# A layer normalisation that streams through SBUF: tiles of 10 rows in a ring of 50 in place of tiles of 8 rows in a ring of 48

## The chip, the cores and the metric

One Trainium2 chip, one core of it. The metric is the time of one execution on the device in microseconds (us), as a median over executions. Engines: DVE (VectorE), ACT (ScalarE), POOL (GpSimd), SP (SyncE), and the core's 16 DMA engines, which carry everything between HBM and SBUF.

## The reference

```python
# x: (32, 512, 1024) float32, eps = 1e-5
mean = np.mean(x, axis=-1, keepdims=True)
var = np.var(x, axis=-1, keepdims=True)
return ((x - mean) / np.sqrt(var + eps)).astype(np.float32)
```

There are 16384 vectors of 1024 floats. "A row" below is one vector in each of the 128 partitions: 128 x 4 KB = 0.5 MB. There are 128 such rows, each loaded once and stored once.

## The kernel before

A tile of K rows is loaded by one DMA into a slot of the ring. DVE takes statistics (two instructions per row), POOL combines them in small instructions, ACT takes the root, DVE the reciprocal. ACT then normalises in place, and one DMA stores the slot. Loads are issued from SP, stores from ACT. A later load into the same slot waits for the store.

```python
TILES = (2, 2, 4) + (8,) * 14 + (4, 2, 2)
RING = 48
GROUP = 8
...
    def rows_of(a, row, K):        # each partition gets K vectors that lie side by side in HBM
        return a[row * P : (row + K) * P].rearrange("(p k) d -> p k d", p=P)
...
    def group(xs, G):
        stats = st.tile([P, GROUP, NSUB, 6], fdt, name="stats")
        for k in range(G):
            for s in range(NSUB):
                nc.vector.bn_stats(out=stats[:, k, s, :], in_=xs[:, k, s * BN_MAX : (s + 1) * BN_MAX])
        ...                        # nine small POOL instructions for all G rows at once
        nc.scalar.activation(out=std[:, :G], in_=ss[:, :G], func=AF.Sqrt, bias=eps_t, scale=1.0 / D)
        nc.vector.reciprocal(out=rstd[:, :G], in_=std[:, :G])
        nc.gpsimd.tensor_mul(out=nmr[:, :G], in0=nmean[:, :G], in1=rstd[:, :G])
        for k in range(G):
            nc.scalar.activation(out=xs[:, k, :], in_=xs[:, k, :], func=AF.Identity,
                                 bias=nmr[:, k : k + 1], scale=rstd[:, k : k + 1])
...
        for K, row, pos in place(TILES, RING):
            nc.sync.dma_start(out=ring[:, pos : pos + K, :], in_=rows_of(x2, row, K))
            for g in range(0, K, GROUP):
                G = min(GROUP, K - g)
                group(ring[:, pos + g : pos + g + G, :], G)
            nc.scalar.dma_start(out=rows_of(o2, row, K), in_=ring[:, pos : pos + K, :])
```

What one partition gets of one tile lies side by side in HBM. In the trace it is one packet of K x 4 KB; a tile is 128 packets, 8 on each DMA engine.

## Time and profile before

| | before |
|---|---|
| time, median (lowest to highest of 3) | 318.12 us (318.04 to 318.23) |
| span in the profile | 316.1 us |
| load queue and store queue, share of 16 engines | 49.6% + 49.3% |
| data packets per DMA engine | 320 |
| first data packet starts, last one ends | 1.76, 314.9 us |

Read the row of the 40 slices first: each digit is the busy share of one fortieth of the span, in tenths. The times of packets are from the trace's packet records. The prediction below shows the lines. The chain of waits gives shares of the span to what was waited for last:

```profile
DMA 58%; DVE 17%; ACT 9%; POOL 6%; issue 3%; another core or an unknown queue 3%; ACTq 0%; POOLq 0%; DVEq 0%; SPq 0%
```

### The profile page before, as it was taken

What the parts mean: (1) busy time and instruction counts of PE and PEld (TensorE: products, weight loads), DVE (VectorE), ACT (ScalarE), POOL (GpSimd) and SP (SyncE); (2) the same over time, 40 slices, a digit from 0 to 9 for tenths busy, and PEclk for the clock granted to TensorE, in tenths of its full rate; (3) what the DMA queues carried; (4) which work ended last, traced back from release to release, by engine and by line L of the source; (5) the groups of instructions that cost most, each with busy time, mean ns of one, the idle gap of its engine ahead of it and who ended that gap; (6) DMA issues with size and microseconds to landing.
All of it is one profiled execution on the core that took longest, in us unless ns stands there. A gap on an engine that the chain in (4) does not pass through costs nothing.

```text
span 316.1 us, 794 instructions
## 1 busy us (share of the span) xinstructions
DVE 157.1 (50%) x277; ACT 154.3 (49%) x149; POOL 45.1 (14%) x204
## 2 busy tenths in 40 slices
DVE  2368596547092561916529074190652908363030
ACT  1336296692833809247091561900651956196321
POOL 0420202201102020020200202002020020221120
DMA  7999999999999999999999999999999999999996
GB/s 301 433 399 469 431 416 425 433 427 444 420 448 419 444 419 444 435 427 444 419 448 415 448 424 440 423 448 419 444 423 440 423 435 429 446 428 417 455 411 282
DMA packets 5766, 134.27 MB, mean 425 GB/s; under 512 B 640, under 2 KB 640, under 8 KB 640
## 3 DMA queue, kind: packets, MB, share of 16 engines
q1 hardware_dynamic: 2880, 67.11, 49.6%
q10 hardware_dynamic: 2880, 67.11, 49.3%
q14 instruction: 6, 0.05, 0.0%
HBM read 67.11 MB, written 67.11 MB: 425 GB/s over the span
## 4 chain that ended last, share of the span: by engine, by line
DMA 58%; DVE 17%; ACT 9%; POOL 6%; issue 3%; another core or an unknown queue 3%; ACTq 0%; POOLq 0%; DVEq 0%; SPq 0%
DMA ring<-in_x_dram 32%; DMA out_dram<-ring 27%; DVE stats L75 17%; ACT ring L111 8%; POOL half L64 1%; ACT std L103 1%; POOL dev L97 1%; POOL nmean L87 1%; POOL dev L100 1%; POOL dev L90 1%; POOL dev L96 1%; POOL nmean L67 1%; POOL ss L67 1%; DVE rstd L107 0%
## 5 line engine op out<-in xcount | busy, mean ns | idle before, releaser
L75 DVE BATCH_NORM_STATS2 stats<-ring 128x6 f32<-128x512 f32 x256 | 153.7, 678 | 71.2 <-DMA ring<-in_x_dram 71.2
L111 ACT ACTIVATE ring<-ring,nmr,rstd 128x1024 f32<-128x1024 f32 x128 | 147.0, 1227 | 10.8 <-POOL nmr L109 10.8
L103 ACT ACTIVATE std<-ss,eps_t 128x8 f32<-128x8 f32 (+2 forms) x20 | 6.0, 300 | 143.0 <-POOL ss L67 115.8
L107 DVE RECIPROCAL rstd<-std 128x8 f32<-128x8 f32 (+2 forms) x20 | 3.9, 193 | 77.3 <-ACT std L103 77.3
L64 POOL TENSOR_TENSOR half<-stats 128x16 f32<-128x16 f32 (+2 forms) x20 | 4.5, 226 | 221.0 <-DVE stats L75 221.0
L109 POOL TENSOR_TENSOR nmr<-nmean,rstd 128x8 f32<-128x8 f32 (+2 forms) x20 | 4.0, 202 | 27.2 <-DVE rstd L107 27.2
L97 POOL TENSOR_SCALAR dev<-dev 128x32 f32<-128x32 f32 (+2 forms) x20 | 5.6, 281 | 1.8
L100 POOL TENSOR_TENSOR dev<-dev,stats 128x32 f32<-128x32 f32 (+2 forms) x20 | 4.9, 243 | 1.7
L90 POOL TENSOR_TENSOR dev<-stats,nmean 128x32 f32<-128x32 f32 (+2 forms) x20 | 4.6, 231 | 1.7
L87 POOL TENSOR_SCALAR nmean<-nmean 128x8 f32<-128x8 f32 (+2 forms) x20 | 4.6, 228 | 1.8
L96 POOL TENSOR_TENSOR dev<-dev 128x32 f32<-128x32 f32 (+2 forms) x20 | 4.6, 228 | 1.6
L64 POOL TENSOR_TENSOR half<-dev 128x16 f32<-128x16 f32 (+2 forms) x20 | 4.2, 210 | 1.6
L67 POOL TENSOR_TENSOR nmean<-half 128x8 f32<-128x8 f32 (+2 forms) x20 | 4.0, 199 | 1.6
L67 POOL TENSOR_TENSOR ss<-half 128x8 f32<-128x8 f32 (+2 forms) x20 | 4.0, 199 | 1.6
L103 ACT ACT_TABLE_LOAD x1 | 1.3, 1283 | 0.9 <-DVE eps_t L120 0.9
L120 DVE MEMSET eps_t<- 128x1 f32 x1 | 0.1, 59 | 0.8 <-PEq L143 0.8
L143 POOL MEMSET const-float32-0.0<- 128x1 f32 x1 | 0.1, 98 | 0.2 <-issue 0.2
L143 POOL MEMSET const-uint8-127<- 128x1 uint8 x1 | 0.1, 102 | 0.0
L143 POOL MEMSET const-bfloat16-1.0<- 128x1 bf16 x1 | 0.1, 101 | 0.0
L143 POOL MEMSET const-float32-1.0<- 128x1 f32 x1 | 0.1, 98 | 0.0
## 6 DMA issues: line engine op xcount, KB each, us to landing
ring<-in_x_dram SPq DMA_DIRECT2D x14, 4096.0 KB, 47.3
out_dram<-ring ACTq DMA_DIRECT2D x14, 4096.0 KB, 40.7
ring<-in_x_dram SPq DMA_DIRECT2D x4, 1024.0 KB, 30.8
ring<-in_x_dram SPq DMA_DIRECT2D x2, 2048.0 KB, 27.2
out_dram<-ring ACTq DMA_DIRECT2D x4, 1024.0 KB, 16.7
out_dram<-ring ACTq DMA_DIRECT2D x2, 2048.0 KB, 24.5
```

Source lines behind the costliest of these rows:

```text
L64: nc.gpsimd.tensor_tensor(out=half[:, :G], in0=terms[:, :, 0:2], in1=terms[:, :, 2:4], op=ALU.add)
L67: nc.gpsimd.tensor_tensor(out=o, in0=half[:, :G, 0], in1=half[:, :G, 1], op=ALU.add)
L75: nc.vector.bn_stats(out=stats[:, k, s, :], in_=xs[:, k, s * BN_MAX : (s + 1) * BN_MAX],)
L87: nc.gpsimd.tensor_scalar(out=nmean[:, :G], in0=nmean[:, :G], scalar1=-1.0 / H, scalar2=None, op0=ALU.mult)
L90: nc.gpsimd.tensor_tensor(out=dev[:, :G], in0=mean4, in1=nmean[:, :G].unsqueeze(2).to_broadcast([P, G, H]), op=ALU.add,)
L96: nc.gpsimd.tensor_mul(out=dev[:, :G], in0=dev[:, :G], in1=dev[:, :G])
L97: nc.gpsimd.tensor_scalar(out=dev[:, :G], in0=dev[:, :G], scalar1=float(D // H), scalar2=None, op0=ALU.mult)
L100: nc.gpsimd.tensor_tensor(out=dev[:, :G], in0=dev[:, :G], in1=m2, op=ALU.add)
L103: nc.scalar.activation(out=std[:, :G], in_=ss[:, :G], func=AF.Sqrt, bias=eps_t, scale=1.0 / D)
L107: nc.vector.reciprocal(out=rstd[:, :G], in_=std[:, :G])
L109: nc.gpsimd.tensor_mul(out=nmr[:, :G], in0=nmean[:, :G], in1=rstd[:, :G])
L111: nc.scalar.activation(out=xs[:, k, :], in_=xs[:, k, :], func=AF.Identity, bias=nmr[:, k : k + 1], scale=rstd[:, k : k + 1],)
```

## The change

The intent: fewer and larger packets, fewer DMAs, one combination of statistics per larger group, and more small buffers, so that nothing waits for one.

```diff
-TILES = (2, 2, 4) + (8,) * 14 + (4, 2, 2)
+TILES = (4, 6, 10, 10, 10, 10, 10, 10, 10, 10, 10, 10, 10, 6, 2)
-RING = 48
+RING = 50
-GROUP = 8
+GROUP = 10
+FINE = 6
+LAST = 3
...
-    st = ctx.enter_context(tc.tile_pool(name="st", bufs=4))
+    st = ctx.enter_context(tc.tile_pool(name="st", bufs=3))
+    sm = ctx.enter_context(tc.tile_pool(name="sm", bufs=10))   # all small tiles but stats move here
...
-        for K, row, pos in place(TILES, RING):
+        for t, (K, row, pos) in enumerate(plan):
             nc.sync.dma_start(out=ring[:, pos : pos + K, :], in_=rows_of(x2, row, K))
-            for g in range(0, K, GROUP):
-                G = min(GROUP, K - g)
+            step = FINE if t >= len(TILES) - LAST else GROUP
+            for g in range(0, K, step):
+                G = min(step, K - g)
                 group(ring[:, pos + g : pos + g + G, :], G)
             nc.scalar.dma_start(out=rows_of(o2, row, K), in_=ring[:, pos : pos + K, :])
```

The last three tiles are handled in groups of at most 6 rows. The plan of slots is computed as before, in line.

More of the change, by code (lines that the diff above doesn't have):

```diff
@@ L7 @@
 from concourse._compat import with_exitstack
-TILES = (2, 2, 4) + (8,) * 14 + (4, 2, 2)
-RING = 48
-GROUP = 8
-def place(tiles, ring):
-    plan, row, pos = [], 0, 0
-    for K in tiles:
-        if pos + K > ring:
-            pos = 0
-        plan.append((K, row, pos))
-        row += K
-        pos += K
-    return plan
+TILES = (4, 6, 10, 10, 10, 10, 10, 10, 10, 10, 10, 10, 10, 6, 2)
[3 more added lines that the diff above has]
+LAST = 3
 @with_exitstack
@@ L45 @@
     NSUB = D // BN_MAX
+    H = 2 * NSUB
     assert sum(TILES) * P == N
     rings = ctx.enter_context(tc.tile_pool(name="rings", bufs=1))
-    st = ctx.enter_context(tc.tile_pool(name="st", bufs=4))
+    st = ctx.enter_context(tc.tile_pool(name="st", bufs=3))
+    sm = ctx.enter_context(tc.tile_pool(name="sm", bufs=10))
     fdt = mybir.dt.float32
@@ L62, in pool_sum @@
         G = terms.shape[1]
-        half = st.tile([P, GROUP, 2], fdt, name="half")
+        half = sm.tile([P, GROUP, 2], fdt, name="half")
         nc.gpsimd.tensor_tensor(
@@ L78, in group @@
                 )
-        H = 2 * NSUB
         parts = stats[:, :G].rearrange("p g s (h c) -> p g (s h) c", h=2)
         mean4, m2 = parts[:, :, :, 1], parts[:, :, :, 2]
-        nmean = st.tile([P, GROUP], fdt, name="nmean")
-        dev = st.tile([P, GROUP, H], fdt, name="dev")
-        ss = st.tile([P, GROUP], fdt, name="ss")
+        nmean = sm.tile([P, GROUP], fdt, name="nmean")
+        dev = sm.tile([P, GROUP, H], fdt, name="dev")
+        ss = sm.tile([P, GROUP], fdt, name="ss")
         pool_sum(nmean[:, :G], mean4)
@@ L101, in group @@
         pool_sum(ss[:, :G], dev[:, :G])
-        std = st.tile([P, GROUP], fdt, name="std")
+        std = sm.tile([P, GROUP], fdt, name="std")
         nc.scalar.activation(
@@ L105, in group @@
         )
-        rstd = st.tile([P, GROUP], fdt, name="rstd")
+        rstd = sm.tile([P, GROUP], fdt, name="rstd")
         nc.vector.reciprocal(out=rstd[:, :G], in_=std[:, :G])
-        nmr = st.tile([P, GROUP], fdt, name="nmr")
+        nmr = sm.tile([P, GROUP], fdt, name="nmr")
         nc.gpsimd.tensor_mul(out=nmr[:, :G], in0=nmean[:, :G], in1=rstd[:, :G])
@@ L117, in group @@
             )
+    plan, row, pos = [], 0, 0
+    for K in TILES:
+        if pos + K > RING:
+            pos = 0
+        plan.append((K, row, pos))
+        row += K
+        pos += K
     with tc.manual_schedule():
         nc.vector.memset(eps_t, eps_val)
-        for K, row, pos in place(TILES, RING):
+        for t, (K, row, pos) in enumerate(plan):
             nc.sync.dma_start(out=ring[:, pos : pos + K, :], in_=rows_of(x2, row, K))
-            for g in range(0, K, GROUP):
-                G = min(GROUP, K - g)
+            step = FINE if t >= len(TILES) - LAST else GROUP
+            for g in range(0, K, step):
+                G = min(step, K - g)
                 group(ring[:, pos + g : pos + g + G, :], G)
```

## The prediction

> **What bounds the kernel now.** The page comes first, and in it the row of the 40 slices, because a busy share over the whole span can hide idle stretches.
>
> ```profile
> span 316.1 us, 794 instructions
> DVE 157.1 (50%) x277; ACT 154.3 (49%) x149; POOL 45.1 (14%) x204
> DMA  7999999999999999999999999999999999999996
> DMA packets 5766, 134.27 MB, mean 425 GB/s; under 512 B 640, under 2 KB 640, under 8 KB 640
> q1 hardware_dynamic: 2880, 67.11, 49.6%
> q10 hardware_dynamic: 2880, 67.11, 49.3%
> ```
>
> No compute engine is over 50%. The DMA digit is 9 in 38 of 40 slices. The load queue (q1) and the store queue (q10) together take 49.6 + 49.3 = 98.9% of sixteen engines' span, that is 312.6 us of 316.1. The traffic, 67.11 MB in and 67.11 MB out, is the least that the task allows, and the change leaves it alone. At most about 3.5 us are to be had from filling idle DMA time, and these must be at the ends. The stretches say where:
>
> ```profile
> 2.00:300.00 298.00, 154.39 (x271) 150.52 (x146) 42.89 (x190) 1.00 1.00 431
> 300.00:310.00 10.00, 2.64 (x5) 2.67 (x3) 2.05 (x10) 1.00 0.97 414
> 310.00:316.10 6.10, 0.00 (x0) 0.00 (x0) 0.00 (x0) 1.00 0.60 251
> ```
>
> The last two columns are DMA share and GB/s. From 2 to 300 us the share is 1.00. In the trace's packet records the first data packet starts at 1.76 us and the last ends at 314.9 us. So 1.76 us of start and 1.2 us after the last byte are fixed, and between them lie 313.1 us. In the last slice one engine ends 1.7 us before another.
>
> The chain of waits names compute (DVE 17%, ACT 9%), and one could be misled by it: those pieces are behind a full transfer queue. The queue's own waits show the same: the largest is for stores that free the ring.
>
> ```profile
> SPq L122 <- DMA out_dram<-ring: 215.6, 12, 19.0
> ```
>
> 215.6 us of waiting in that queue cost nothing as long as the DMA share is 1.00. The timeline of the end shows how the two queues share the engines:
>
> ```profile
> 276.54 4.85 DVE L75 BATCH_NORM_STATS2 stats<-ring 128x6 f32<-128x512 f32 x8 [1.52 <-DMA ring<-in_x_dram]
> ...
> 288.65 2.48 DVE L75 BATCH_NORM_STATS2 stats<-ring 128x6 f32<-128x512 f32 x4 [3.24 <-DMA ring<-in_x_dram]
> ...
> 300.78 2.47 DVE L75 BATCH_NORM_STATS2 stats<-ring 128x6 f32<-128x512 f32 x4 [6.54 <-DMA ring<-in_x_dram]
> ...
> 309.08 0.34 ACTq L126 DMA_DIRECT2D out_dram<-ring  x1
> ```
>
> The last two loads, of 2 rows, land 12.11 and 12.13 us apart. The packet records have medians of 309, 611 and 1213 ns for packets of 8, 16 and 32 KB, and each engine has 8 packets in a load. Eight turns of one load packet of 8 KB and one store packet of 32 KB make 8 x (309 + 1213) = 12.2 us. So the queues take turns packet by packet, not byte by byte. The last store is issued at 309.08, while the store before it, by the records, is still moving until 310.8 to 312.4. The tail is bound by transfers too; compute beats it by about 2 us.
>
> **What the Trainium skill says.** "DMA: Bandwidth & Descriptors", section "Queues, rings and completion order": each DMA engine goes round robin over its queues at packet granularity. The trace agrees (12.2 worked out, 12.1 measured). Section "Where 436 GB/s comes from" of the same page: 16 ports x 32 B x 850 MHz = 435.2 GB/s. A 32 KB packet in 1213 ns on 16 engines is 432 GB/s, so the kernel stands at that limit. Section "Anatomy of one DMA — SWDGE (gpsimd) path" gives some 2 us of fixed cost per DMA, most of it the receipt of the last write; these DMAs are of the other kind (hardware queues)[...]. In the middle, share 1.00, it is covered by other transfers. "HBM Reference", section "Specifications (TRN2)": a core alone measures about 425 GB/s, bounded by its DMA engines. The page of this kernel shows 425 GB/s.
>
> **The change, part by part.** There are two ledgers: work on the DMA engines, which sets the time, and compute, which matters only if a queue runs dry.
>
> *Packets.* Before: 20 tiles, 8 packets per engine each way, 320 data packets per engine (64 of 8 KB, 32 of 16, 224 of 32). After: 15 tiles, 240 packets. The durations 309, 611, 1213 lie on a line: about 301 ns per 8 KB and 8 ns per packet. An estimate on that line is 912 ns for 24 KB and 1515 for 40 KB. Before: 64 x 309 + 32 x 611 + 224 x 1213 = 311.0 us per engine. After: 16 x 309 + 16 x 611 + 32 x 912 + 176 x 1515 = 310.5 us (4.9 + 9.8 + 29.2 + 266.6). Gain 0.6 us. Completion writes (9 ns each, 40 per engine before, 30 after) give 0.1 us. Sum: -0.7 us.
>
> *The start.* The first tile has 4 rows in place of 2. Its load takes 2.4 us longer, so it lands near 8.1 us (5.69 before). Its 8 statistics take 4.8 us, the chain to the first normalisation 3.4 us (8.16 to 11.58 in the timeline before) and four normalisations 4.6 us, so the first store is issued near 21 us, not at 13.99. This costs nothing if loads fill the engines: the first five loads have no wait, 40 rows x 1.21 us = 48 us of work (one row of all partitions is 301.3 x 8 / 2 = 1.21 us), the sixth waits only for the first load's semaphore, and the seventh needs the stores of the 4-row and 6-row tiles. The second store is issued near 33 us, and turn by turn (8 x (611 + 1515), then 8 x (912 + 1515)) both have landed near 60 us. By then some 37 of the 50 rows first granted are in. The load queue has 13 rows left and does not run dry.
>
> *The middle.* A 10-row tile in both directions takes 8 x 2 x 1.515 = 24.2 us. DVE needs 12.0 us of statistics plus 3.3 us of idling for its own reciprocal, ACT 11.8 us. Both have 9 us to spare. From landing to store issue: 12.0 + 3.7 + 11.5 = 27.2 us (the 8-row tile took 9.6 + 3.7 + 9.2 = 22.5, 37.51 to 60.03). Five tiles give 121 us per turn of the ring against 24 + 27 + 24 = 75 us needed. The ring is looser per row in neither kernel, and nothing starves. The combined statistics take 10 POOL instructions from 20 groups to 16, some 2.6 us each, off the path. The additional small buffers remove waits that were not seen.
>
> *The tail.* With a load landing every 24.2 us, the last 10-row tile (halves of 6 and 4) lands near 261 us. Its successors' packets of 24 and 8 KB alternate with store packets of 40 KB: 8 x (912 + 1515) = 19.4 us and 8 x (309 + 1515) = 14.6 us, so the loads end near 295 us. Stores end near 290 (last but three), 303, 310 and 312.5 us; they are issued near 264, 284, 298 and 303. Each is issued 5 to 26 us before its turn. Compute stays ahead, with more slack than the 2 us of before.
>
> Sum: 318.1 - 0.7 = 317.4 us.
>
> **The rivals.** *Fewer DMAs pay their fixed cost less often.* Ten DMAs fewer at 2 us would make 298 us, 6% faster. Against it stands the share of 1.00 between 2 and 300 us: such a cost would be idle time there, and only 3.5 us of idling exist. I give it 1%. *The coarser grain opens gaps* (late first store, five slots, 27 us from landing to store): a dry store queue alone costs nothing, since loads then take every turn; both must be dry. If the load queue ran dry before the second store came back, some 5 us would be lost (323); if the tail's last two stores came late, 3 to 5 us. My steps leave 13 rows and 5 us of slack, so 2% for more than 6 us. *Load-only stretches are slower*: the records show load packets of 32 KB at a mean of 1274 ns between 10 and 20 us after the first packet, around the first stores' issue, against 1213 later. This cost the mean engine about 0.75 us. The load-only stretch is longer after, so this could grow by 0.3 to 0.6 us and eat the gain: 317.9. *Packets of 40 KB* could be split or move slower than the line says; 1% on them is 2.7 us (320). Speed near the limit and linearity from 8 to 32 KB speak against it.
>
> **Range and chances.** 317.4 us; the rival of slow load stretches and the 1.7 us spread of the engines at the end make some +-0.8, runs of one kernel spread by 0.2. So 316.7 to 318.5. Faster by over 2% (below 311.8) would need less than the bytes' own time at the limit, 310.7 + 1.8 + 1.2 + 2.0 outside the span = 315.7: 1%. Slower by over 2% (above 324.5): 2%. Within: 97%.
>
> **What would show it right or wrong.** Right: DMA 9 in all inner slices, q1 and q10 with 2160 packets each and together 98 to 99% of a span near 315.4; 40 KB packets near 1515 ns; the first store near 21 us; the last loads 14.6 us apart; the last store issued before its predecessor ends. Wrong: a slice below 9 between the second and the 38th, 40 KB packets far from 1515 ns, or a last store that waits for its normalisation with idle engines.

## The result

318.03 us median (317.89 to 318.50, 4 runs) against 318.18 us (318.04 to 318.56, 4 runs). The ratio is 0.9996, with a 95% interval of 0.9979 to 1.0014: the same. Ratios here are the mean time of one kernel's fast runs over that of the other's fast runs in the same rounds, so not quite the ratio of the medians. The profiled execution was the slowest of the four (318.50).

The page of the changed kernel, the lines that answer to those shown of before:

```profile
span 316.6 us, 712 instructions
DVE 156.5 (49%) x273; ACT 152.6 (48%) x145; POOL 37.5 (12%) x164
DMA  8999999999999999999999999999999999999995
DMA packets 4324, 134.25 MB, mean 424 GB/s; under 512 B 480, under 2 KB 480, under 8 KB 480
q1 hardware_dynamic: 2160, 67.11, 49.6%
q10 hardware_dynamic: 2160, 67.11, 49.1%
DMA 42%; DVE 26%; another core or an unknown queue 14%; POOL 6%; ACT 5%; issue 3%; SPq 0%; DVEq 0%; POOLq 0%
```

The packets of each queue fell from 2880 to 2160, and the digits are 9 in 38 of 40 slices again. The chain of waits now gives DVE 26% where it had 17%, at the same time: that view follows one of several ways back through a full queue. Stretches of the same kernel (columns: stretch, its length, DVE, ACT and POOL busy time, clock, DMA share, GB/s):

```profile
2.00:300.00 298.00, 156.31 (x271) 148.91 (x142) 36.39 (x156) 1.00 1.00 431
300.00:310.00 10.00, 0.17 (x1) 2.67 (x3) 0.91 (x5) 1.00 0.99 428
310.00:316.60 6.60, 0.00 (x0) 0.00 (x0) 0.00 (x0) 1.00 0.46 192
```

From 2 to 300 us the engines moved 431 GB/s, exactly as before. The timeline of the end:

```profile
261.86 7.21 DVE L68 BATCH_NORM_STATS2 stats<-ring 128x6 f32<-128x512 f32 x12 [8.69 <-DMA ring<-in_x_dram]
...
281.24 7.22 DVE L68 BATCH_NORM_STATS2 stats<-ring 128x6 f32<-128x512 f32 x12 [0.89 <-DMA ring<-in_x_dram]
...
295.89 2.47 DVE L68 BATCH_NORM_STATS2 stats<-ring 128x6 f32<-128x512 f32 x4 [4.12 <-DMA ring<-in_x_dram]
...
304.19 0.34 ACTq L127 DMA_DIRECT2D out_dram<-ring  x1
```

The last two loads land 14.65 us apart (14.6 predicted from packets that take turns). The last store is issued at 304.19, while by the packet records the store before it ends between 310.6 and 312.8 on the different engines. The last bytes end at 315.2.

So the result lay in the predicted range, and 0.6 us above its point of 317.4. The range also holds 318.1 to 318.2, the time of no change at all, so lying in it is no sign of a gain. What was to be found out: is compute really off the path, is it packets or DMAs that cost, when do the ends and the ring begin to matter, and where is the 0.7 us that the ledger of packets had promised?

### The profile page after: what moved, and what is told of

Its sections match the earlier page's. It is cut to its first block, busy times and chain, and to the rows that moved or that the text cites. A ratio compares the mean times of both kernels' runs of the same rounds, so it can differ in the third digit from the quotient of the medians.

```text
span 316.6 us, 712 instructions
## 1 busy us (share of the span) xinstructions
DVE 156.5 (49%) x273; ACT 152.6 (48%) x145; POOL 37.5 (12%) x164
## 3 DMA queue, kind: packets, MB, share of 16 engines
q1 hardware_dynamic: 2160, 67.11, 49.6%
q10 hardware_dynamic: 2160, 67.11, 49.1%
## 4 chain that ended last, share of the span: by engine, by line
DMA 42%; DVE 26%; another core or an unknown queue 14%; POOL 6%; ACT 5%; issue 3%; SPq 0%; DVEq 0%; POOLq 0%
DMA ring<-in_x_dram 29%; DVE stats L68 26%; DMA out_dram<-ring 13%; ACT ring L103 4%; POOL half L57 1%; POOL dev L89 1%; ACT std L95 1%; POOL dev L92 1%; POOL dev L82 1%; POOL nmean L79 1%; POOL dev L88 1%; POOL nmean L60 1%; POOL ss L60 1%; DVE rstd L99 0%
## 5 line engine op out<-in xcount | busy, mean ns | idle before, releaser
L95 ACT ACTIVATE std<-ss,eps_t 128x10 f32<-128x10 f32 (+3 forms) x16 | 4.8, 301 | 141.7 <-POOL ss L60 141.7
L57 POOL TENSOR_TENSOR half<-stats 128x20 f32<-128x20 f32 (+3 forms) x16 | 3.7, 233 | 243.2 <-DVE stats L68 243.2
L99 DVE RECIPROCAL rstd<-std 128x10 f32<-128x10 f32 (+3 forms) x16 | 3.3, 204 | 51.7 <-ACT std L95 51.7
L89 POOL TENSOR_SCALAR dev<-dev 128x40 f32<-128x40 f32 (+3 forms) x16 | 4.6, 289 | 1.4
L101 POOL TENSOR_TENSOR nmr<-nmean,rstd 128x10 f32<-128x10 f32 (+3 forms) x16 | 3.3, 205 | 10.4 <-DVE rstd L99 10.4
L92 POOL TENSOR_TENSOR dev<-dev,stats 128x40 f32<-128x40 f32 (+3 forms) x16 | 4.1, 259 | 1.3
L79 POOL TENSOR_SCALAR nmean<-nmean 128x10 f32<-128x10 f32 (+3 forms) x16 | 3.9, 244 | 1.4
L82 POOL TENSOR_TENSOR dev<-stats,nmean 128x40 f32<-128x40 f32 (+3 forms) x16 | 3.9, 245 | 1.3
L88 POOL TENSOR_TENSOR dev<-dev 128x40 f32<-128x40 f32 (+3 forms) x16 | 3.8, 239 | 1.3
L57 POOL TENSOR_TENSOR half<-dev 128x20 f32<-128x20 f32 (+3 forms) x16 | 3.4, 212 | 1.3
```

The source lines that it names most:

```text
L57: nc.gpsimd.tensor_tensor(out=half[:, :G], in0=terms[:, :, 0:2], in1=terms[:, :, 2:4], op=ALU.add)
L79: nc.gpsimd.tensor_scalar(out=nmean[:, :G], in0=nmean[:, :G], scalar1=-1.0 / H, scalar2=None, op0=ALU.mult)
L82: nc.gpsimd.tensor_tensor(out=dev[:, :G], in0=mean4, in1=nmean[:, :G].unsqueeze(2).to_broadcast([P, G, H]), op=ALU.add,)
L88: nc.gpsimd.tensor_mul(out=dev[:, :G], in0=dev[:, :G], in1=dev[:, :G])
L89: nc.gpsimd.tensor_scalar(out=dev[:, :G], in0=dev[:, :G], scalar1=float(D // H), scalar2=None, op0=ALU.mult)
L92: nc.gpsimd.tensor_tensor(out=dev[:, :G], in0=dev[:, :G], in1=m2, op=ALU.add)
```

## The experiments

All kernels but one computed the right result; the exception: dma_only. Its output is wrong, which doesn't matter for the time. Each was run beside the kernel before on the same chip.

### after_again: the changed kernel in five rounds

No edit.

> The changed kernel once more, in five rounds against the kernel before, because the measured difference (0.15 us) is inside the noise of four runs. Theory A (the ledger of the prediction): the transfer work falls by 0.7 us per DMA engine, but the start, in which load packets wait on their first bytes, and the lag of the slowest DMA engine at the end take most of it back, so 317.8 to 318.2 us against 318.1 to 318.2. Rival B (four runs hid it): the full 0.7 us shows, 317.4 us.

Measured: 318.24 us (318.20 to 318.29, 5 runs), before 318.10 us (11 runs), ratio 1.0005 (0.9993 to 1.0017). Rival B falls: no gain of 0.7 us was hidden by the few runs. The median is 0.04 us above the upper end of theory A's range.

### dma_only: the transfers without the arithmetic

```diff
-            step = FINE if t >= len(TILES) - LAST else GROUP
-            for g in range(0, K, step):
-                G = min(step, K - g)
-                group(ring[:, pos + g : pos + g + G, :], G)
```

> The changed kernel without any statistics or normalisation: the same 30 transfers, each store waiting for its load alone. The result is wrong on purpose. Theory A: compute is wholly off the path, so 317.3 to 318.3 us, less than 1 us below the changed kernel. Rival C (compute is on the path, as the 26% of DVE in the chain of waits suggests): 3 us or more below, 315 or less.

Measured: 317.59 us (316.98 to 319.40, 6 runs), ratio 0.9993 (0.9974 to 1.0013). Its page:

```profile
span 316.1 us, 95 instructions
DVE 0.1 (0%) x1; POOL 0.2 (0%) x4
DMA  8999999999999999999999999999999999999995
```

With 157 us of DVE and 153 us of ACT taken out, the time is the same within the noise: its median is 0.65 us below the 318.24 of the changed kernel, and its own runs differ by 2.4. The 26% of DVE in the chain of waits was no cost. Counted from the lower end of this interval to the changed kernel's 1.0005, no change to its arithmetic can gain more than about 1 us.

### group5: the combined statistics undone

```diff
-            step = FINE if t >= len(TILES) - LAST else GROUP
+            step = FINE if t >= len(TILES) - LAST else 5 if K == GROUP else GROUP
```

> Undoes the combined statistics: each 10-row tile is handled as two groups of 5 rows, with everything else kept. Theory A: compute lies behind a full transfer queue, so the same time within 0.3 us, 317.8 to 318.3. Rival C: the longer chain of small instructions per group matters; 11 more chains of some 3.7 us, at least 1 us of it visible, over 319.

Measured: 318.33 us (318.30 to 318.78, 5 runs), ratio 1.0010 (0.9998 to 1.0022); the changed kernel had 318.24. Combining ten rows at once bought nothing that could be measured, and rival C falls here too. (The median is 0.03 us above theory A's interval.)

### packets8k and packets4k: the same DMAs, smaller packets

```diff
 # packets4k (packets8k deals the rows out in pairs)
-        return a[row * P : (row + K) * P].rearrange("(p k) d -> p k d", p=P)
+        return a[row * P : (row + K) * P].rearrange("(k p) d -> p k d", p=P)
```

Number and size of the DMAs, tiles, ring and groups stay; only how the rows are dealt to the partitions differs, and with it the length of a contiguous run.

> The tiles, the ring, the groups and the count of DMAs of the changed kernel, but the rows are dealt to partitions two at a time, so that each DMA is made of packets of 8 KB instead of up to 40 KB. Theory A (8 ns per packet, nothing per DMA): 1024 packets per engine at 309 ns are 316.4 us against 310.5, so plus 5.9 us: 323.9, between 322.5 and 325. Rival D (what counts is the number and size of DMAs, not of packets): unchanged, 318.

> The same with packets of 4 KB, one row each. Theory A: 2048 packets per engine at an estimated 158.5 ns (150.5 of bytes and 8) are 324.6 us, so plus 14.1 us: 332, between 329 and 335. Rival D: unchanged, 318. A third case, that short packets are moved several at a time: less than plus 8 us.

Measured: 321.83 us (321.69 to 321.92) and 327.05 us (326.97 to 327.25), 4 runs each, ratios 1.0110 and 1.0276. The stretch from 100 to 250 us of each, first before, then after, 8 KB, 4 KB:

```profile
100.00:250.00 150.00, 74.91 (x131) 72.35 (x69) 16.42 (x71) 1.00 1.00 433
```

```profile
100.00:250.00 150.00, 77.53 (x134) 70.34 (x66) 14.80 (x61) 1.00 1.00 434
```

```profile
100.00:250.00 150.00, 75.30 (x131) 70.35 (x66) 14.64 (x60) 1.00 1.01 428
```

```profile
100.00:250.00 150.00, 73.08 (x127) 70.34 (x66) 14.64 (x60) 1.00 1.02 422
```

The DMA share stays full while the rate falls: 433 and 434 for large packets, 428, 422. So rival D (only DMAs count) falls; packets cost something. But theory A had the size wrong: both times are below its intervals. From 8 to 4 KB there are 1024 more packets per engine and 5.22 us more, 5.1 ns each. From the changed kernel (318.24) to 8 KB there are 784 more and 3.6 us, 4.6 ns each. It is about 5 ns, not the 8 ns that the durations gave. The share above 1.00 fits that: 0.01 of 309 ns and 0.02 of 159 ns are some 3 ns per packet (an estimate) in which recorded packets overlap. A line through durations (4 KB packets took 159 ns, as estimated) counts the overlap as cost. One thing was not separated: the edit also changes the HBM addresses that one packet and its neighbours cover, so the 5 ns may hold a cost of that order of access too.

### rows16: packets of 64 KB

```diff
-TILES = (4, 6, 10, 10, 10, 10, 10, 10, 10, 10, 10, 10, 10, 6, 2)
+TILES = (4, 4, 8, 16, 16, 16, 16, 16, 16, 8, 4, 2, 2)
-RING = 50
+RING = 48
-GROUP = 10
+GROUP = 8
```

> Takes the packet step further: bulk tiles of 16 rows (64 KB packets) in a ring of 48 rows, groups of 8, fine tiles at both ends. On the line of 8 ns per packet and 301.3 ns per 8 KB the data packets of one engine take 310.06 us, 0.4 less than the changed kernel. Theory A: the ends stay as large as they were or grow with the packet, so 317.3 to 318.5. Rival (fixed cost per DMA): 4 DMAs fewer, minus 8 us, 310. Rival (three slots of 16 rows are too few: load 38.7 + compute about 36 + store 38.7 = 113 us against 116 us per turn): gaps, over 321.

Measured: 325.60 us as the median of 5 fast runs (325.3 to 329.7; 325.97 with the slow one), ratio 1.0273 (1.0233 to 1.0314): slower. Its slices and the stretch around 80 us:

```profile
DMA  7999989989899989989999999899998989999995
```

```profile
78.00:86.00 8.00, 6.46 (x11) 6.45 (x6) 1.13 (x5) 1.00 0.69 266
```

Theory A and the fixed cost per DMA both miss; the rival of too few slots has it. At 82.90 SP issues the next load, after the store that frees the slot; around it the DMA share is 0.69, and near 200 us, one turn of the ring later, there is another dip. By the packet records the three 16-row slots took 118, 119 and 130 us from one landing to the next, against 116 us of transfers per turn. One thing the rival's account did not contain: up to the first dip three small stores (packets of 16 and 32 KB) took turns with load packets of 64 KB and so came home late. That share in the dip was read off, not tested alone.

### ring30 and ring20: how many slots does it take?

```diff
-RING = 50
+RING = 30        # ring20: 20
```

> The changed kernel with a ring of 30 rows, three tiles instead of five. Theory A: the turn of the ring takes 3 x 24.2 = 72.7 us of transfers; a tile needs about 12.1 + 27 + 12.1 = 51 us where the other queue is empty. So the engines seldom run dry: 318 to 322. Rival G (each slot needs 24 + 27 + 24 = 75 us as in the prediction's account, more than 72.7): plus 3% of the middle, 327 or more.

> A ring of 20 rows, two tiles. Theory A: now both queues are dry at times. Two tiles take at least 51 us plus two landings and two starts of about 1.5 us, some 54 us, against 48.4 us of transfers: 11 to 13% over the middle, 345 to 360 us, with DMA digits clearly below 9. Rival (the ring is as good as irrelevant): under 325.

Measured: 337.33 us (336.40 to 339.10), ratio 1.0605, and 365.87 us (365.49 to 366.43), ratio 1.1494; 4 runs each. The slices of ring30, then of ring20:

```profile
DMA  8999997999999997999999997999999999799997
```

```profile
DMA  8996898989798897998986989968998989889947
```

Both of my intervals were too low. In ring30 the dips come about every 79 us: by the packet records, loads that take the same slot land at 47, 129, 205 and 284 us. So the account that the prediction used (24 + 27 + 24 = 75 us per slot, rival G) is right in kind and 3.6 us short. From the packet and issue records, a turn in ring30 takes 78.6 us as a mean of seven: 22.9 of load, 27.8 from landing to store issue, 21.6 of store, and 6.4 of hand-overs, that is from a DMA's issue to its first packet (2.4 for the load, 3.6 for the store) and from a store's last packet to the next load's issue (0.5). Three tiles have 72.7 us of transfers. My argument that the queues help each other failed: load and store took 20 to 26 us each, not near 12.

From 130.3 to 131.8 us both queues are dry, because the next store is not normalised yet (issued at 132.90) and the next load was only issued at 130.87. The two issues, and the stretch (columns as in the stretches above):

```profile
130.87 0.33 SPq L122 DMA_DIRECT2D ring<-in_x_dram  x1
132.90 0.34 ACTq L127 DMA_DIRECT2D out_dram<-ring  x1
128.00:133.00 5.00, 3.64 (x7) 4.87 (x5) 0.00 (x0) 1.00 0.71 238
```

For ring20 the reading, both queues dry at times, was right, and its size 6 us short of the time measured. The same records give a turn of 56.2 us where some 54 were expected: the hand-overs are 2.3 (0.9 to a first packet twice, and 0.5), and the load takes 13.7, not 12.1. In the load issued at 99.20, the engines' first packets of 40 KB took 1.5 to 3.0 us each, all later ones but one 1.51. So most of the miss is a slow start of each load; the first packets were looked at in this one load only.

By the same rule five slots of 10 rows (121 us per turn) have some 40 us to spare, and six of 8 rows before (116 us) some 50.

### coarse_start, coarse_end and fine_start_coarse_end: the ends

```diff
-TILES = (4, 6, 10, 10, 10, 10, 10, 10, 10, 10, 10, 10, 10, 6, 2)
+TILES = (10, 10, 10, 10, 10, 10, 10, 10, 10, 10, 10, 10, 6, 2)     # coarse_start
+TILES = (10, 10, 10, 10, 10, 10, 10, 10, 10, 10, 10, 10, 8)        # coarse_end, with LAST = 0
+TILES = (4, 6, 10, 10, 10, 10, 10, 10, 10, 10, 10, 10, 10, 8)      # fine_start_coarse_end, with LAST = 0
```

> The tiles of 4 and 6 rows at the start become one tile of 10 rows. The first store can then only be issued near 1.8 + 12.1 + 1 + 12.0 + 3.7 + 11.5 = 42 us instead of 21.6. Theory A: loads fill the engines meanwhile, the time stays within 0.5 us of the changed kernel, 317.5 to 318.5. Rival E (a late first store is lost time, half of the 20 us because loads run on): 328.

> As coarse_start, and the tiles of 6 and 2 rows at the end become one tile of 8 rows with its statistics in one group. Theory A: after the last load nothing but its own store is left, and it comes 22.5 us after the landing plus about 1.3 us to its first packet, while the stores before it keep the engines busy for only about 20.4 us: a gap of 3.4 us, so 321.4, between 319.5 and 323.5. Rival F (the end is as indifferent as the middle): 318.

Measured: coarse_start 318.32 us (ratio 1.0002), coarse_end 318.15 us (ratio 0.9995), 4 runs each. The first was as theory A said: a first store some 20 us later costs nothing. The second was a miss. The last load had landed by 274.67, not near the 284 that the changed kernel's last loads would give (worked out in the next text), and the last store was issued at 297.20. My expectation had taken the stores still owed at the end from the changed kernel. With a late first store the loads run ahead, they are all done 10 us earlier, and what is owed then is stores, which cover the last tile. This new reading was put to the test by keeping the fine start:

> Run coarse_end lost nothing, because its late start had let the loads run ahead and the stores owed at the end then covered the last tile (last load landed at 274.7, last store issued at 297.2, its predecessor still moving until 302.5 to 304.4). This run keeps the fine start (4 and 6 rows) of the changed kernel and makes only the end coarse: one last tile of 8 rows in one group. From the trace of the changed kernel: the last full load lands at 261.9, eight turns of 1213 + 1514 ns make 21.8, so the last load lands near 283.7; 22.5 us on, at 306.2, the last store is issued, first packet near 307.5. All other transfers are done near 314.9 - 9.7 = 305.2. Theory A: a gap of 2.3 us, 320.4, between 319.3 and 321.5, with DMA idle near 306. Rival (the end is indifferent for another reason): 318.2.

(In that text, 302.5 to 304.4 for the predecessor's end is a slip in the origin of time: it is 303.5 to 305.4.) Measured: 321.16 us (321.01 to 321.33, 4 runs), ratio 1.0091 (1.0076 to 1.0107). The last store's issue and the stretches, of coarse_end, then of fine_start_coarse_end:

```profile
297.20 0.34 ACTq L127 DMA_DIRECT2D out_dram<-ring  x1
290.00:300.00 10.00, 0.00 (x0) 7.17 (x7) 0.00 (x0) 1.00 1.01 438
300.00:310.00 10.00, 0.00 (x0) 0.00 (x0) 0.00 (x0) 1.00 0.99 428
```

```profile
306.97 0.34 ACTq L127 DMA_DIRECT2D out_dram<-ring  x1
290.00:300.00 10.00, 4.25 (x8) 2.52 (x3) 2.32 (x10) 1.00 0.94 406
300.00:310.00 10.00, 0.00 (x0) 6.94 (x7) 0.00 (x0) 1.00 0.57 244
310.00:319.20 9.20, 0.00 (x0) 0.00 (x0) 0.00 (x0) 1.00 0.80 342
```

ACT still normalises in the second kernel's stretch from 300 to 310 us, and the DMA share there is 0.57; its last store was issued at 306.97 (306.2 expected), after the store before it had ended at 305.0 by the packet records. In the first, ACT is done before 300 and the share is 0.99. The two programs have the same last tile. They differ in their first 10 rows.

### before_again: a second trace of the kernel before

No edit to the kernel before.

> The kernel before once more, for a second trace of it. The data stretch (first to last packet) was 313.1 us before and 313.2 to 313.5 in two traces after, though after has 80 packets per engine fewer. Theory A (the true cost of a packet is the 5 ns that the 4 KB and 8 KB runs show, so 0.4 us was to be had, and a lag of the slowest engine at the end that differs from run to run hides it): the lag between first and last engine at the end lies again between 1.6 and 2.2 us and the data stretch between 313.0 and 313.7. Rival (the larger packets of the changed kernel lengthen that lag): 1.7 us or less here, as in the first trace.

Measured: 318.08 us (4 runs), ratio 0.9996. By the packet records of this trace the data stretch is 313.5 us and the lag between the first and the last engine at the end 2.0 us. The traces of the changed kernel have 313.5 and 313.2 us, and lags of 2.2 and 2.0. The rival's sign did not come: with 1.7 and 2.0 before, no clearly longer lag is seen with larger packets. Nor is after_again's theory A borne out where it had the lag take back the gain.

## Why the prediction was right

The measured 318.03 lies in the range of 316.7 to 318.5, and "within 2%" was right. That the transfers bound both kernels was right as a mechanism; the gain of 0.7 us was not seen, and that the range held is partly its width. By its own steps:

- **The transfers bound the kernel.** Shown: dma_only takes 317.59 us with no arithmetic.
- **Fewer DMAs save no fixed cost in the middle (the first rival).** Shown: 30 DMAs take the time of 40. Of the 1.3 us after the last byte (315.2 to a span of 316.55), which the prediction calls fixed, only some 0.4 pass until SP's wait for the last store ends at 315.60; the rest is the program's own closing instructions, not a cost of a DMA.
- **The start costs nothing.** The first store was issued at 21.58 us (near 21 predicted), the second at 34.28 (near 33), both had landed at 63.6 (near 60). Coarse_start doubled the delay at no cost.
- **The middle has room.** Right, and ring30 shows how far: the account of 75 us per slot was 3.6 us short, with 6.4 us of hand-overs that it left out and transfers 4 us shorter. (Landing to store issue took 27.8 us, 27.2 predicted; by the prediction's own figures ACT had 12 us to spare per tile, not 9.)
- **The tail.** Stores ended by the packet records at 278.0, 293.1, 305.5, 312.8 and 315.2 us; the last four were predicted at 290, 303, 310 and 312.5. Those figures fit the engine that ends first (290.6, 303.4, 310.6 and 313.1); the last engine is 2 to 2.5 us behind. They were issued at 264.94, 285.32, 299.01 and 304.19 (264, 284, 298, 303). Each was thus issued before its turn.
- **The step that was mis-sized: "301 ns per 8 KB and 8 ns per packet", hence -0.7 us.** 40 KB packets did take 1514 ns (1515 predicted). Its own sums, 311.0 and 310.5, differ by 0.5, not by the 0.6 written, so its ledger gave 0.6 in all. But the cost of a packet is about 5 ns by the runs with short packets, so 80 packets fewer were worth 0.4 us.
- **The step that left something out: ends taken as unchanged.** The table gives, from the packet records, the time less the bytes moved by then at 301.2 ns per 8 KB and engine, so what was lost up to that moment.

| lost up to | before, two traces | changed, two traces | packets8k | packets4k |
|---|---|---|---|---|
| 12 us | 2.7, 2.7 | 2.9, 2.9 | 2.9 | 3.2 |
| 290 us | 5.1, 5.0 | 5.0, 4.8 | 8.2 | 12.7 |

Between the two moments the changed kernel loses 0.2 to 0.5 us less, which fits 0.4; in the first 12 us it loses 0.2 more. The slow first packets of the first load are there in both. Why they cost more in the changed kernel stays open, for coarse_start and coarse_end, with even larger first packets, lost 2.8 and 2.7. The rest is inside the 0.3 us by which traces of one kernel differ. Net, 0 to 0.3 us remain of the promised 0.7, and the runs can't tell them from zero.
- **The rival of slow load-only stretches.** Its sign was there: packets of 40 KB had a mean of 1690 ns in the third stretch of 10 us after the first packet. Yet it cost nothing. Between 12 and 60 us the changed kernel lost 1.1 and 0.8 us, the kernel before 1.1 twice. Those slow load packets lie where the first store begins, each long by about the first store's packet (some 2.15 us, where 1.51 and 0.61 make 2.12). It fits that the two records overlap on an engine and count one time twice; the records kept carry no engine, so this is argued, not shown.

No variant with the right result beat both kernels. With 309 us of bytes at the 434 GB/s of the middle, some 1.7 us to the first packet, 1.3 us after the last byte and about 2 us outside the span, the floor of this way of streaming on this core is near 314 us (an estimate from these numbers). Both kernels stand some 4 us, a little over 1%, above it.

## What to carry to other kernels

When the DMA digit is 9 from end to end and the bytes cannot fall, as here, look for no more than tenths of a microsecond from tile size, ring and combined statistics; taking the arithmetic out as an experiment shows this in one run. They start to matter when a slot's load, compute, store and hand-overs exceed the transfer time of one turn of the ring (78.6 against 72.7 us in ring30), or when the last tile's arithmetic outlasts the stores still owed. And read the cost of a packet from two kernels that differ in packets, not from durations of records that overlap.

## What the Trainium skill lacked or had wrong

- "DMA: Bandwidth & Descriptors", section "Why small descriptors are slow (HBM only)": it gives about 3 cycles of overhead per packet and 32 bytes of descriptor metadata per DMA operation, but no time for runs of kilobytes. Here the cost was 4.6 to 5.1 ns per contiguous run, and runs of 4 KB took 2.8% longer than the kernel before with runs of 8 to 32 KB.
- The same page, "Queues, rings and completion order": it has the turns per packet, but says that an engine drains a packet of typically 9 to 17 descriptors from one queue before it switches. In these traces a packet is one contiguous run (up to 64 KB), and the queues alternate run by run, so queues with unlike runs share unequally. A load of 1 MB in 8 KB packets beside 40 KB store packets landed 14.65 us after the load before it.
- The same page, "Anatomy of one DMA — SWDGE (gpsimd) path": its sum of about 2 us per DMA is for the GpSimd path. For DMAs from SP and ACT on an idle queue, ring20 shows 0.8 to 1.0 us from issue to first packet and 0.4 to 0.6 us from the last packet to the next issue that waited for it; with both queues full no cost per DMA is seen (40 and 30 DMAs, 318.1 and 318.2 us).
- No page has what a slot of a ring needs: its load, compute and store at the shared rate, plus hand-overs of some 6 us in ring30. Three slots were short by 6 us per turn, and the time grew by 6%.
